# A layer's first two transfers cut anew: norm weights, one weight tile and the left half of x first

## The chip, the cores and the metric

The kernel runs on one core of a Trainium2 chip. The metric is the device time of one execution in microseconds (us). Besides it there is one profiled execution, with its own time and a span from the first to the last instruction.

## The reference, cut to what matters

One layer of a hybrid encoder: x is 512 positions by 1024 features, float32.

```python
h = rms_norm(x, attn_norm_g)
xr, gate, q, k, v = split(h @ w_in)             # 2560 columns
y_rnn  = (rg_lru(conv(xr), fwd) + rg_lru(conv(xr), bwd)) * gelu(gate)
y_attn = dilated_attention(q, k, v, rel_bias)   # 8 heads, three windows
x = x + concat(rms_norm(y_rnn), rms_norm(y_attn)) @ w_out
x = x + square(relu(rms_norm(x) @ w_up)) @ w_down
return rms_norm(x, final_norm_g)
```

The change concerns the start: x times the norm weights `attn_norm_g`, and the first columns of `w_in` (those of `xr`), which are multiplied first. The row's own factor 1/sqrt(mean(x^2)) is applied later, to the products.

## The kernel before, in words

**Products in three passes.** Each float32 operand is split into a rounded part (`hi`) and the rest (`lo = value - hi`), both held in a type that TensorE multiplies at full pace. A product is hi*hi + hi*lo + lo*hi, three matmuls into the same bank (`mm3`, L311 to L314). ScalarE mostly does the rounding, VectorE the subtraction.

**Row tiles.** x comes transposed: 8 row tiles of 128 features, each 128 partitions by 512 positions. With row tile k come rows of `w_in`: 3 weight tiles of 128 columns (the first 384 columns of `xr`), side by side in one piece of memory, so that one transfer brings both: 512 + 384 = 896 columns (`xw`, L341). Row tile 0 has its own array `xw0` with the 8 columns of norm weights between x and the weights, and comes in two transfers: x and norm weights (520 columns, L335), then the three weight tiles (384, L336). A fourth weight tile (columns 384 to 511) is needed early for row tile 0 alone; it comes from `w_in[3]` by a third transfer of 128 columns (`w03`, L339). All of these are issued by the Sync queue (SP) in the order of the code; `vt` (small vectors) and row tile 7 follow.

**`cvx(k)`** (L347) scales x by the norm weights and rounds it into `h_hi`, rounds the weights into `w3h`, and subtracts both to get `h_lo` and `w3l`. For row tiles 0 and 1 the work is shared: for row tile 0 ScalarE rounds the left 256 columns of x (L353) and VectorE the right 256 (L354), VectorE two weight tiles (L356) and ScalarE the third (L357), then the fourth (L366). `sq(k)` (L370) squares x on ScalarE for the row sums, `addsq` (L374) adds the squares on VectorE. Each engine takes its instructions in the order in which the code calls them.

**TensorE** begins with 8 matmuls on a constant (`pwarm`, L141), two instructions each, whose result nobody uses. Then, at L448 to L460, four banks `pxr[0..3]` gather the products. For row tiles 0 and 1 the passes are the outer loop: first hi*hi of weight tiles 0, 1, 2, then hi*lo of the three, then lo*hi (L453); for row tile 0 the fourth bank follows (L455, with the lines of `mm3`). From row tile 2 on, `mm3` per tile. After that come the gates, the attention with its tables, the output projection, and the two halves of the large feed-forward part with streamed weights.

**The end.** `fg` (final norm weights) is read into `fgt[0]` and `fgt[1]`, 128 partitions each, in pieces of partitions given by `FGP` (L1356, issue at L1725): 3 pieces and 4.

Of the kernel before, what the change touches and what calls it, by code (L numbers as in the profile page):

```python
# [35 lines left out]
TH = S // 2  # L36
# [62 lines left out]
def hybrid_kernel(ctx: ExitStack, tc, xw0, xw, xn, w_in, w_v, w_out, w_up, w_dn, gates, vecs, bias, fg, out):  # L99
    nc = tc.nc  # L100
# [3 lines left out]
    work = ctx.enter_context(tc.tile_pool(name="work", bufs=1))  # L104
# [17 lines left out]
    def f(t):  # L122
        return t.bitcast(FT)
# [14 lines left out]
    act(warm, epsb, AF.Exp)  # L138
    pwarm = ps_("pwarm", "et")
    one = nc.const_aps.tensor(1.0, [P, P], FT)  # L140
    for _ in range(8):  # L141
        nc.tensor.matmul(pwarm[:, :P], lhsT=one, rhs=one, start=True, stop=True)

    def softplus_consts():
# [166 lines left out]
    def mm3(o, a, b, first, last, on=False):  # L311
        nc.tensor.matmul(o, lhsT=a[0], rhs=b[0], start=bool(first), stop=False, skip_group_check=on)  # L312
        nc.tensor.matmul(o, lhsT=a[0], rhs=b[1], start=False, stop=False, skip_group_check=on)  # L313
        nc.tensor.matmul(o, lhsT=a[1], rhs=b[0], start=False, stop=bool(last), skip_group_check=on)  # L314
# [8 lines left out]
    h_hi = big.tile([P, KD, S], FR, name="h_hi", tag="bigA")  # L323
    h_lo = big.tile([P, KD, S], FR, name="h_lo", tag="bigB")

    XW, XG = S + 3 * P, S + KD
    ag = consts.tile([P, KD], FT, name="ag")
    xwt, w3 = [], []
    for k in range(KD):
        if 4 <= k < 7:  # L330
            xwt.append(stream.tile([P, 1024], FT, name="wraw", tag="wraw", bufs=3)[:, :XW])
        else:
            xwt.append(work.tile([P, 1024], FT, name="tw", tag="tw", bufs=4)[:, :XW if k else XG + 3 * P])
        if k == 0:
            nc.sync.dma_start(xwt[0][:, :XG], xw0[:, :XG])  # L335
            nc.sync.dma_start(xwt[0][:, XG:], xw0[:, XG:])  # L336
            nc.gpsimd.tensor_copy(ag, xwt[0][:, S:XG])
            w03 = g_("w03")[:, :P]
            nc.sync.dma_start(w03, w_in[3][:, :P])  # L339
        else:  # L340
            nc.sync.dma_start(xwt[k], xw[k - 1])  # L341
        if k == 6:
            nc.sync.dma_start(vt, vecs)

    sqx = {}

    def cvx(k):  # L347
        x, w = xwt[k][:, :S], xwt[k][:, S if k else XG:]
        g = ag[:, k:k + 1] if k else xwt[0][:, S:S + 1]
        hi, lo = g_("w3h", FR), g_("w3l", FR)  # L350
        if k < 2:
            c = (2 * P, 3 * P)[k]
            act(h_hi[:, k, :c], x[:, :c], AF.Copy, scale=g)  # L353
            nc.vector.tensor_scalar(h_hi[:, k, c:], x[:, c:], g, None, op0=OP.mult)  # L354
            if k == 0:
                nc.vector.tensor_copy(hi[:, :2 * P], w[:, :2 * P])  # L356
                act(hi[:, 2 * P:3 * P], w[:, 2 * P:], AF.Copy)  # L357
            else:
                nc.vector.tensor_copy(hi[:, :3 * P], w)
        else:  # L360
            act(h_hi[:, k, :], x, AF.Copy, scale=g)
            act(hi[:, :3 * P], w, AF.Copy)
        stt(h_lo[:, k, :], x, g, f(h_hi)[:, k, :], op0=OP.mult, op1=OP.subtract)
        nc.vector.tensor_tensor(lo[:, :3 * P], w, f(hi)[:, :3 * P], op=OP.subtract)
        if k == 0:
            act(hi[:, 3 * P:], w03, AF.Copy)  # L366
            nc.vector.tensor_tensor(lo[:, 3 * P:], w03, f(hi)[:, 3 * P:], op=OP.subtract)
        w3.append((hi, lo))

    def sq(k):  # L370
        sqx[k] = g_("sqx")
        act(sqx[k], xwt[k][:, :S], AF.Square)

    def addsq(k):  # L374
        nc.vector.tensor_tensor(sqx[0], sqx[0], sqx.pop(k), op=OP.add)
# [72 lines left out]
    pxr = {t: ps_("pxr", "pj") for t in range(4)}  # L448
    for k in range(KD):
        if k < 2:  # L450
            for i, (a, b) in enumerate(((0, 0), (0, 1), (1, 0))):
                for t in range(3):
                    nc.tensor.matmul(pxr[t], lhsT=wk(t, k)[a], rhs=hk(k)[b], start=i == 0 and k == 0, stop=False)  # L453
            if k == 0:
                mm3(pxr[3], wk(3, 0), hk(0), True, False)  # L455
            continue
        for t in range(3):
            mm3(pxr[t], wk(t, k), hk(k), False, k == KD - 1)
            if k == KD - 1 and t == 0:
                sqt = turned(sqx[0], "et")  # L460

# [797 lines left out]
    for w in OSEQ:  # L1259
        for i in range(4):  # L1260
            tt, k = i // 2, i % 2
# [260 lines left out]
    for half in range(2):  # L1522
# [5 lines left out]
        start = 0  # L1528
        if half == 0:
            start = 3  # L1530
# [286 lines left out]
```

## Time and profile before

| | us |
|---|---|
| median of 3 runs | 525.29 (525.0 to 525.39) |
| profiled execution, its time | 525.49 |
| profiled execution, its span | 523.7 |
| TensorE (PE) busy | 517.1 (99% of the span) |
| VectorE (DVE) busy | 430.4 (82%) |
| ScalarE (ACT) busy | 352.2 (67%) |
| GpSimd (POOL) busy | 65.3 (12%) |

The time is that of the execution; the span runs from its first to its last instruction, 1.8 us less. PE stands for TensorE's matmuls, PEld for its weight loads, which run beside them, SP for the Sync engine, whose q marks its issuing queue. In a row of the timeline the first number is the start in us from the span's start, the second the duration, then engine, line, operation, and output<-inputs by the program's names; `x3` says that three like instructions were merged, and a bracket names idle time in front and what ended it. A matmul row's duration holds its way through the array, so two rows overlap, and the pace is read from one start to the next. Where a helper records every operation, the line is that of the helper (L312 to L314).

### The profile page before, as it was taken

To read this page: it belongs to the slowest core of one execution; us is meant where nothing else is said; L and a number is where in the kernel's file an instruction comes from. 1 tells how busy PE (TensorE), PEld (TensorE's weight loads), DVE (VectorE), ACT (ScalarE), POOL (GpSimd) and SP (SyncE) were. 2 spreads that over 40 slices of the span, in tenths; PEclk is the share of its full clock that TensorE was granted. 3 is DMA by queue.
4 is the path that set the end of the run, shared out by engine and by line. 5 is a ranking of instruction groups with operands and counts; after the bars stand their busy time and mean duration, and the time that the engine had idled before them with its cause. 6 is when DMAs were issued, how large, how long until landed. Compare 5 with 4: busy or idle time off the path is not lost.

```text
span 523.7 us, 8216 instructions
## 1 busy us (share of the span) xinstructions
PE 517.1 (99%) x3021; PEld 444.3 (85%) x3021; DVE 430.4 (82%) x668; ACT 352.2 (67%) x570; POOL 65.3 (12%) x89
## 2 busy tenths in 40 slices
PE   9999999999999999999999999999999999999995
PEld 8867888778777788899999888889999999888884
DVE  6899986788886898898789987789766978986885
ACT  7579946667857857586578666565667577655655
POOL 0173000000000321001300312001100300131000
PEclk9999999999999999999999999999999999999999
DMA  7636555266796499947595899976986497799704
GB/s 288 208 99 196 161 160 180 83 191 199 190 294 197 115 196 247 353 134 195 139 223 143 213 273 281 306 271 161 300 256 168 117 224 210 157 289 257 195 1 161
DMA packets 40329, 105.15 MB, mean 201 GB/s; under 512 B 5056, under 2 KB 13376, under 8 KB 40288
## 3 DMA queue, kind: packets, MB, share of 16 engines
q1 hardware_dynamic: 32448, 78.10, 44.5%
q0 software_dynamic: 7696, 26.32, 27.3%
q8 instruction: 24, 0.39, 0.3%
q10 hardware_dynamic: 144, 0.20, 0.1%
q14 instruction: 17, 0.14, 0.1%
HBM read 95.59 MB, written 4.29 MB: 191 GB/s over the span
## 4 chain that ended last, share of the span: by engine, by line
PE 99%; DVE 0%; issue 0%; DVEq 0%; ACT 0%; ACTq 0%
PE pu L314 10%; PE pu L312 10%; PE pu L313 10%; PE pd L314 10%; PE pd L312 10%; PE pd L313 10%; PE pqk L312 3%; PE pqk L314 3%; PE pqk L313 3%; PE pwo L312 3%; PE pwo L314 3%; PE pwo L313 3%; PE pav L942 2%; PE pt L842 2%; PE ps L806 2%; PE pp L312 1%
## 5 line engine op out<-in xcount | busy, mean ns | idle before, releaser
L269 DVE TENSOR_TENSOR wlo<-wraw,whi 128x1024 fp32r<-128x1024 f32 x71 | 86.6, 1220 | 24.0 <-ACT whi L247 23.9
L247 ACT ACTIVATE whi<-wraw 128x1024 fp32r<-128x1024 f32 x67 | 70.8, 1057 | 37.4 <-PE pd L314 18.4
L313 PE MATMUL pd<-wlo,ah 128*128 128x512 f32 (+1 forms) x195 | 75.2, 386 | 0.0
L312 PE MATMUL pd<-whi,ah 128*128 128x512 f32 (+1 forms) x195 | 75.2, 386 | 0.0
L314 PE MATMUL pd<-whi,al 128*128 128x512 f32 (+1 forms) x195 | 75.2, 386 | 0.0
L313 PE MATMUL pu<-hl,whi 128*128 128x256 f32 x224 | 63.4, 283 | 0.0
L314 PE MATMUL pu<-hh,wlo 128*128 128x256 f32 x224 | 63.4, 283 | 0.0
L312 PE MATMUL pu<-hh,whi 128*128 128x256 f32 x224 | 63.4, 283 | 0.0
L312 PE MATMUL pu<-h2h,whi 128*128 128x256 f32 (+1 forms) x200 | 60.1, 300 | 0.0
L313 PE MATMUL pu<-h2l,whi 128*128 128x256 f32 (+1 forms) x200 | 60.0, 300 | 0.0
L314 PE MATMUL pu<-h2h,wlo 128*128 128x256 f32 (+1 forms) x200 | 60.0, 300 | 0.0
L269 DVE TENSOR_TENSOR wlo<-tw,whi 128x1024 fp32r<-128x1024 f32 x37 | 45.2, 1221 | 17.7 <-ACT whi L247 17.7
L247 ACT ACTIVATE whi<-tw 128x1024 fp32r<-128x1024 f32 x38 | 40.1, 1058 | 24.9 <-PE pd L314 6.3
L312 PEld LDWEIGHTS pu<-hh,whi 128*128 128x128 f32 x224 | 43.0, 192 | 0.0
L313 PEld LDWEIGHTS pu<-hl,whi 128*128 128x128 f32 x224 | 43.0, 192 | 0.0
L314 PEld LDWEIGHTS pu<-hh,wlo 128*128 128x128 f32 x224 | 43.0, 192 | 0.0
L313 PEld LDWEIGHTS pd<-wlo,ah 128*128 128x128 f32 x195 | 36.6, 188 | 7.4
L312 PEld LDWEIGHTS pd<-whi,ah 128*128 128x128 f32 x195 | 36.6, 188 | 7.3
L314 PEld LDWEIGHTS pd<-whi,al 128*128 128x128 f32 x195 | 36.6, 188 | 7.4
L247 ACT ACTIVATE whi<-ts 128x1024 fp32r<-128x1024 f32 x24 | 25.4, 1060 | 25.2 <-PE pd L314 16.4
L313 PEld LDWEIGHTS pu<-h2l,whi 128*128 128x128 f32 x200 | 38.3, 191 | 1.3
L314 PEld LDWEIGHTS pu<-h2h,wlo 128*128 128x128 f32 x200 | 38.3, 191 | 1.3
(280 smaller groups left out, 1220.1 us busy)
## 6 DMA issues: line engine op xcount, KB each, us to landing
wraw<-in_w_up_dram SPq DMA_DIRECT2D x25, 512.0 KB, 4.8
ts<-in_w_dn_dram POOLq DMA_DIRECT2D x24, 512.0 KB, 13.5
wraw<-in_w_dn_dram SPq DMA_DIRECT2D x24, 512.0 KB, 8.7
tw<-in_w_up_dram SPq DMA_DIRECT2D x15, 512.0 KB, 6.7
tw<-in_w_up_dram POOLq DMA_DIRECT2D x15, 512.0 KB, 7.5
wraw<-in_w_in_dram SPq DMA_DIRECT2D x13, 512.0 KB, 4.3
ts<-in_w_dn_dram SPq DMA_DIRECT2D x8, 512.0 KB, 9.0
tw<-in_w_dn_dram SPq DMA_DIRECT2D x8, 512.0 KB, 7.0
```

Of the source, the lines that this page charges most:

```text
L247: act(hi, raws[i], AF.Copy)
L269: nc.vector.tensor_tensor(lo, r, f(splits[i][0]), op=OP.subtract)
L312: nc.tensor.matmul(o, lhsT=a[0], rhs=b[0], start=bool(first), stop=False, skip_group_check=on)
L313: nc.tensor.matmul(o, lhsT=a[0], rhs=b[1], start=False, stop=False, skip_group_check=on)
L314: nc.tensor.matmul(o, lhsT=a[1], rhs=b[0], start=False, stop=bool(last), skip_group_check=on)
L806: nc.tensor.matmul(psq[p, u][e][:, :NK], lhsT=qs_[p, a][r, P * qt:P * qt + P], rhs=kks[p][r, b, w:w + NK], start=i == 0, stop=i == 2)
L842: nc.tensor.transpose(pt[:, i * P:(i + 1) * P], en[h][qt][:, k:k + P], ident)
L942: nc.tensor.matmul(pav[p][a, co], lhsT=vs[:, jt, h * DH:(h + 1) * DH], rhs=et[h, jt][:, ci], start=jt == 0 and i == 0, stop=jt == 3 and i ...
```

## The change

Row tile 0's array is put in another order and its transfers are cut elsewhere. The first transfer now brings the norm weights, weight tile 0 and the left half of x (8 + 128 + 256 = 392 columns), the second the right half of x and weight tiles 1 and 2 (512 columns). The fourth weight tile of row tile 0 is appended to row tile 1's transfer (1024 columns instead of 896), and its own transfer goes. `cvx(0)` deals its work out anew: VectorE rounds the left half of x, ScalarE weight tile 0, VectorE tiles 1 and 2, ScalarE the right half; the subtractions are made for each half of x and for tile 0 and tiles 1 and 2 apart. `cvx(1)` gets the rounding and subtraction of the fourth tile ahead of its own. The hi*hi products of row tile 0 are made by column halves: the left 256 columns of weight tiles 0, 1, 2, then the right 256. There are 7 warm-up matmuls instead of 8, and `fgt[0]` is read in 4 pieces instead of 3. In the code P is 128, S is 512, TH is 256 and KD is 8; `lr` holds the two column halves; the line numbers of the changed kernel are 5 to 14 higher from here on.

```diff
-    for _ in range(8):
+    for _ in range(7):
...
-    XW, XG = S + 3 * P, S + KD
+    XW, X0 = S + 3 * P, KD + P
+    XL, XR = X0 + TH, X0 + S + 2 * P
...
-            nc.sync.dma_start(xwt[0][:, :XG], xw0[:, :XG])
-            nc.sync.dma_start(xwt[0][:, XG:], xw0[:, XG:])
-            nc.gpsimd.tensor_copy(ag, xwt[0][:, S:XG])
-            w03 = g_("w03")[:, :P]
-            nc.sync.dma_start(w03, w_in[3][:, :P])
+            nc.sync.dma_start(xwt[0][:, :XL], xw0[:, :XL])
+            nc.sync.dma_start(xwt[0][:, XL:], xw0[:, XL:XR])
+            nc.gpsimd.tensor_copy(ag, xwt[0][:, :KD])
+        elif k == 1:
+            nc.sync.dma_start(xwt[1], xw0[:, XR:])
...
+        if k == 0:
+            wa, wb = xwt[0][:, KD:X0], xwt[0][:, X0 + S:]
+            nc.vector.tensor_scalar(h_hi[:, k, lr[0]], x[:, lr[0]], g, None, op0=OP.mult)
+            act(hi[:, :P], wa, AF.Copy)
+            nc.vector.tensor_copy(hi[:, P:3 * P], wb)
+            act(h_hi[:, k, lr[1]], x[:, lr[1]], AF.Copy, scale=g)
+            for c in lr:
+                stt(h_lo[:, k, c], x[:, c], g, f(h_hi)[:, k, c], op0=OP.mult, op1=OP.subtract)
+            nc.vector.tensor_tensor(lo[:, :P], wa, f(hi)[:, :P], op=OP.subtract)
+            nc.vector.tensor_tensor(lo[:, P:3 * P], wb, f(hi)[:, P:3 * P], op=OP.subtract)
+        elif k == 1:
+            c = 3 * P
+            w03, hi0, lo0 = xwt[1][:, XW:], w3[0][0][:, c:], w3[0][1][:, c:]
+            act(hi0, w03, AF.Copy)
             act(h_hi[:, k, :c], x[:, :c], AF.Copy, scale=g)
             nc.vector.tensor_scalar(h_hi[:, k, c:], x[:, c:], g, None, op0=OP.mult)
...
+            nc.vector.tensor_tensor(lo0, w03, f(hi0), op=OP.subtract)
+            nc.vector.tensor_copy(hi[:, :3 * P], w)
...
+                if i == k == 0:
+                    for c in lr:
+                        for t in range(3):
+                            nc.tensor.matmul(pxr[t][:, c], lhsT=wk(t, 0)[0], rhs=hk(0)[0][:, c], start=c is lr[0], stop=False, skip_group_check=True)
+                    continue
...
-    FGP = ((0, 32, 64, 128), (0, 32, 64, 96, 128))
+    FGP = ((0, 32, 64, 96, 128), (0, 32, 64, 96, 128))
```

TensorE's queue at the start, before (`pwarm` is the warm-up, `w3h` and `w3l` the rounded weights and their rest, `h_hi` and `h_lo` the same of x, `pxr` the banks; in brackets the engines or transfers whose semaphores a row waits for):

```order
L142 MATMUL pwarm<-const-float32-1.0 128x128 x8
L453 MATMUL pxr<-h_hi,w3h 128x512 [waits DVE_49,Activation_49]
L453 MATMUL pxr<-h_hi,w3h 128x512
L453 MATMUL pxr<-h_hi,w3h 128x512 [waits Activation_49]
L453 MATMUL pxr<-h_lo,w3h 128x512 [waits DVE_49]
L453 MATMUL pxr<-h_lo,w3h 128x512 x2
L453 MATMUL pxr<-h_hi,w3l 128x512 [waits DVE_49]
L453 MATMUL pxr<-h_hi,w3l 128x512 x2
L312 MATMUL pxr<-h_hi,w3h 128x512 [waits Activation_49]
L313 MATMUL pxr<-h_lo,w3h 128x512
L314 MATMUL pxr<-h_hi,w3l 128x512 [waits DVE_49]
```

and now:

```order
L142 MATMUL pwarm<-const-float32-1.0 128x128 x7
L464 MATMUL pxr<-h_hi,w3h 128x256 [waits DVE_49,Activation_49]
L464 MATMUL pxr<-h_hi,w3h 128x256 [waits DVE_49]
L464 MATMUL pxr<-h_hi,w3h 128x256
L464 MATMUL pxr<-h_hi,w3h 128x256 [waits Activation_49]
L464 MATMUL pxr<-h_hi,w3h 128x256 x2
L467 MATMUL pxr<-h_lo,w3h 128x512 [waits DVE_49]
L467 MATMUL pxr<-h_lo,w3h 128x512 x2
L467 MATMUL pxr<-h_hi,w3l 128x512 [waits DVE_49] x2
L467 MATMUL pxr<-h_hi,w3l 128x512
L312 MATMUL pxr<-h_hi,w3h 128x512 [waits Activation_49]
L313 MATMUL pxr<-h_lo,w3h 128x512
```

Three products of 512 columns have become six of 256, of which the first waits for VectorE and ScalarE once, the second for VectorE again and the fourth for ScalarE again; the passes behind them stand as they stood.

ScalarE's queue, before (`tw` and `w` are what the transfers brought, `ag` the copied norm weights, `sqx` the squares; DMAHW0, 1, 2 and so on are the Sync transfers in the order of issue):

```order
L353 ACTIVATE h_hi<-tw 128x256 [waits DMAHW0_49]
L357 ACTIVATE w3h<-tw 128x128 [waits DMAHW1_49]
L366 ACTIVATE w3h<-w_102 128x128 [waits DMAHW2_49]
L372 ACTIVATE sqx<-tw 128x512
L353 ACTIVATE h_hi<-tw,ag 128x384 [waits DMAHW3_49,Pool_49]
L372 ACTIVATE sqx<-tw 128x512
L361 ACTIVATE h_hi<-tw,ag 128x512 [waits DMAHW4_49]
L362 ACTIVATE w3h<-tw 128x384
```

and now:

```order
L356 ACTIVATE w3h<-tw 128x128 [waits DMAHW0_49]
L358 ACTIVATE h_hi<-tw 128x256 [waits DMAHW1_49]
L381 ACTIVATE sqx<-tw 128x512
L366 ACTIVATE w3h<-tw 128x128 [waits DMAHW2_49]
L367 ACTIVATE h_hi<-tw,ag 128x384 [waits Pool_49]
L381 ACTIVATE sqx<-tw 128x512
L372 ACTIVATE h_hi<-tw,ag 128x512 [waits DMAHW3_49]
L373 ACTIVATE w3h<-tw 128x384
```

The fourth weight tile's rounding (L366) stood ahead of the squares of row tile 0 and waited for a transfer of its own; it stands behind them now and waits for row tile 1's transfer, in front of that tile's own rounding.

The Sync queue, before (the row's last number is the transfer's partitions by columns):

```order
L335 DMA tw<-in_xw_dram 128x520
L336 DMA tw<-in_xw_dram 128x384
L339 DMA w_102<-in_w_in_dram 128x128
L341 DMA tw<-in_xw_dram 128x896 x3
L341 DMA wraw<-in_xw_dram 128x896 x3
L343 DMA vt<-in_vecs_dram 128x60
L341 DMA tw<-in_xw_dram 128x896
```

and now:

```order
L336 DMA tw<-in_xw_dram 128x392
L337 DMA tw<-in_xw_dram 128x512
L340 DMA tw<-in_xw_dram 128x1024
L342 DMA tw<-in_xw_dram 128x896 x2
L342 DMA wraw<-in_xw_dram 128x896 x3
L344 DMA vt<-in_vecs_dram 128x60
L342 DMA tw<-in_xw_dram 128x896
```

One issue has gone, and row tile 1's transfer is the third instead of the fourth.

More of the change, by code (lines that the diff above doesn't have):

```diff
@@ L362, in cvx @@
             act(hi[:, :3 * P], w, AF.Copy)
[L363 to L367, printed above, removed]
+        if k:
+            stt(h_lo[:, k, :], x, g, f(h_hi)[:, k, :], op0=OP.mult, op1=OP.subtract)
+            nc.vector.tensor_tensor(lo[:, :3 * P], w, f(hi)[:, :3 * P], op=OP.subtract)
         w3.append((hi, lo))
@@ L371, in sq @@
         sqx[k] = g_("sqx")
-        act(sqx[k], xwt[k][:, :S], AF.Square)
+        act(sqx[k], xwt[k][:, :S] if k else xwt[0][:, X0:X0 + S], AF.Square)
     def addsq(k):
@@ L451, in hybrid_kernel @@
             for i, (a, b) in enumerate(((0, 0), (0, 1), (1, 0))):
+                if i == k == 0:
[3 more added lines that the diff above has]
+                    continue
                 for t in range(3):
-                    nc.tensor.matmul(pxr[t], lhsT=wk(t, k)[a], rhs=hk(k)[b], start=i == 0 and k == 0, stop=False)
+                    nc.tensor.matmul(pxr[t], lhsT=wk(t, k)[a], rhs=hk(k)[b], start=False, stop=False, skip_group_check=True)
             if k == 0:
@@ L457, in hybrid_kernel @@
         for t in range(3):
-            mm3(pxr[t], wk(t, k), hk(k), False, k == KD - 1)
+            mm3(pxr[t], wk(t, k), hk(k), False, k == KD - 1, True)
             if k == KD - 1 and t == 0:
```

20 lines of the change are left out of this document (7 added, 13 removed).

## The prediction

> **What bounds the kernel now.** I read the page first (engine shares, then the chain that ended last), then TensorE's waits, then the first 16 us of the timeline, because every edit but one lies there, and last the groups by line and the DMA issues for durations.
>
> ```profile
> span 523.7 us, 8216 instructions
> PE 517.1 (99%) x3021; PEld 444.3 (85%) x3021; DVE 430.4 (82%) x668; ACT 352.2 (67%) x570; POOL 65.3 (12%) x89
> ...
> PE 99%; DVE 0%; issue 0%; DVEq 0%; ACT 0%; ACTq 0%
> ```
> TensorE is busy for 517.1 of 523.7 us and 99% of the chain that ended last is its own work. So what ends last is TensorE's queue from its first instruction to nearly its last; whatever makes that queue start its real products earlier shifts everything behind it, and nothing else does.
>
> ```profile
> PE pwarm L142 <- PEq L1806: 0.8, 1, 0.8
> PEld pxr L453 <- ACT w3h L357: 0.2, 1, 0.2
> ```
> The first row is the only wait of TensorE's matmul side in the whole span (0.8 us, before the warm-up). The second is the one wait of its weight loads at the place of the change: 0.2 us on the first rounded weight tile. Now the start itself (start, duration, engine, line):
>
> ```profile
> 0.73 0.39 SPq L335 DMA_DIRECT2D tw<-in_xw_dram  x1
> 0.77 3.75 PE L142 MATMUL pwarm<-const-float32-1.0 128*128 128x128 f32 x16 [0.77 <-PEq L1806]
> 1.18 0.41 SPq L336 DMA_DIRECT2D tw<-in_xw_dram  x1
> 1.64 0.42 SPq L339 DMA_DIRECT2D w<-in_w_in_dram  x1
> ...
> 3.50 0.36 DVE L354 TENSOR_SCALAR h_hi<-tw 128x256 fp32r<-128x256 f32 x1 [2.65 <-DMA tw<-in_xw_dram]
> 3.50 0.51 ACT L353 ACTIVATE h_hi<-tw 128x256 fp32r<-128x256 f32 x1 [1.27 <-DMA tw<-in_xw_dram]
> ...
> 4.00 0.31 ACT L357 ACTIVATE w3h<-tw 128x128 fp32r<-128x128 f32 x1
> 4.00 0.29 DVE L356 CAST w3h<-tw 128x256 fp32r<-128x256 f32 x1
> 4.21 0.74 DVE L363 SCALAR_TENSOR_TENSOR h_lo<-tw,h_hi 128x512 fp32r<-128x512 f32 x1
> 4.41 0.93 PEld L453 LDWEIGHTS pxr<-h_hi,w3h 128*128 128x128 f32 x3 [0.18 <-ACT w3h L357]
> 4.44 1.62 PE L453 MATMUL pxr<-h_hi,w3h 128*128 128x512 f32 x3
> ...
> 5.30 0.31 ACT L366 ACTIVATE w3h<-w 128x128 fp32r<-128x128 f32 x1 [0.99 <-DMA w<-in_w_in_dram]
> ...
> 5.64 0.29 DVE L367 TENSOR_TENSOR w3l<-w,w3h 128x128 fp32r<-128x128 f32 x1 [0.22 <-ACT w3h L366]
> 5.85 1.34 PE L453 MATMUL pxr<-h_lo,w3h 128*128 128x512 f32 x3
> ...
> 6.50 0.62 ACT L353 ACTIVATE h_hi<-tw,ag 128x384 fp32r<-128x384 f32 x1 [0.38 <-DMA tw<-in_xw_dram]
> ...
> 7.03 0.84 PE L453 MATMUL pxr<-h_hi,w3l 128*128 128x512 f32 x3
> ...
> 7.71 0.39 PE L312 MATMUL pxr<-h_hi,w3h 128*128 128x512 f32 x1
> ...
> 8.39 0.84 PE L453 MATMUL pxr<-h_hi,w3h 128*128 128x512 f32 x3
> ```
> The reader is to see three things. First, x and the norm weights arrive at 3.50, the weights at 4.00, and the first real weight load goes out at 4.41, 0.1 us behind the rounding that ended at 4.31 (4.00 + 0.31). Second, TensorE is slow here: the three products of 512 columns that begin at 4.44 give way to the next three at 5.85, and three later ones take 7.03 to 7.71, 0.227 us each. Third, from 5.85 on no row stands behind a wait.
>
> ```profile
> L142 PEld LDWEIGHTS pwarm<-const-float32-1.0 x16: 286/333/333, 0.7 to 3.9; 128*128 128x128 f32 x16
> L142 PE MATMUL pwarm<-const-float32-1.0 x16: 421/421/551, 0.8 to 4.1; 128*128 128x128 f32 x16
> L453 PEld LDWEIGHTS pxr<-h_hi,w3l x6: 187/188/277, 6.7 to 10.0; 128*128 128x128 f32 x6
> ```
> The weight loads tell when the slow time ends: 333 ns in the warm-up, 277 ns for the load at 6.71, 187 ns after it. The products show the same: if two of the three that begin at 5.85 take a slow step and the third a mixed one, the change of pace is at about 6.85. A slow step is 0.43 us (5.85 less 4.44 is 1.41 for three, of which about 0.14 is the first load's fill), nearly twice 0.227. The warm-up is sixteen instructions from 0.8 to 4.1, so 0.22 apart: eight matmuls end at about 4.3, seven at about 3.87.
>
> **The change part by part.**
>
> *The first two transfers.* The first shrinks from 260 KB (520 columns) to 196 KB (392), the second grows from 192 KB to 256 KB (512). Together both are 904 columns, as before.
>
> ```profile
> tw<-in_xw_dram SPq DMA_DIRECT2D x1, 260.0 KB, 2.7
> tw<-in_xw_dram SPq DMA_DIRECT2D x1, 192.0 KB, 2.8
> w<-in_w_in_dram SPq DMA_DIRECT2D x1, 64.0 KB, 3.6
> 2.50:3.50 1.00, 1.00 (x7) 1.00 (x7) 0.00 (x0) 0.00 (x0) 0.00 (x0) 1.00 1.03 360
> ```
> In the stretch in which they arrive the DMA engines are full (share 1.03) and move 360 GB/s. So 64 KB less is 65,536 / 360,000 = 0.18 us: the first lands so that its readers start at 3.32 instead of 3.50. The second ends with the same total byte, and I take 4.00 for its readers, as now. Its bounds: 0.18 later (bigger packets, started no earlier) and 0.2 earlier (it starts as much earlier as the first ends).
>
> *The first product.* ScalarE rounds the first weight tile (0.31, as L357) from 3.32 to 3.63, VectorE the left half of x (0.36, as L354) to 3.68. With one warm-up matmul less TensorE is free at 3.87. So the first half product (256 columns, half of 0.43: 0.21 cold) runs from about 3.9 to 4.1. The second and third need the two tiles that VectorE rounds at 4.00 (0.29, as L356) to 4.29; their load goes out at 4.41, just where the first one stands now. So TensorE arrives at 4.41 with one of six half products behind it: a lead of 0.21 us in slow time. From there the rest is the same work: five halves and then the same chain. Splitting three products into six adds three weight loads; I take nothing for them, because in the warm-up loads follow each other every 0.22 us beside matmuls as short as these halves. If they did not hide, they would cost up to 3 x 0.33 us less the 0.21 of each that streams, 0.36 slow us.
>
> *What the lead is worth.* Slow time ends at 6.85 as now. 0.21 us of slow stream is half a product, and at the full pace half a product is 0.227 / 2 = 0.11 us. That is the gain, and it holds to the end only if nothing behind it is late. That is checked next, each with the new need 0.2 us earlier before 6.85 and 0.11 after.
>
> *The other rounding of tile 0.* ScalarE does the right half of x (0.51, as L353) from 4.00 to 4.51; the fourth half product needs it at 4.57 + 2 x 0.21 = 4.99. VectorE now has two subtractions of 256 columns instead of one of 512 (0.74):
>
> ```profile
> L1473 DVE SCALAR_TENSOR_TENSOR x1n<-pd,r,x1n x1: 484/484/484, 516.8 to 516.8; 128x256 f32<-128x256 f32 x1
> L1476 DVE TENSOR_TENSOR tw<-x1n,fgt x1: 414/414/414, 517.6 to 517.6; 128x256 f32<-128x256 f32 x1
> ```
> At 0.48 each they end at 5.25, needed at about 5.64; then 0.29 (128 columns, as L367) to 5.54 and 0.41 (256) to 5.95, needed at 5.64 + 3 x 0.43 = 6.92. Slack 0.4 and 1.0 us.
>
> *The fourth tile in row tile 1's transfer.* The 64 KB transfer goes (one issue of 0.42 us on the Sync queue); its bytes ride in the next one, issued at 1.64 instead of 2.11, so by bytes that one lands no later than now (readers at 6.50). Rounding and subtraction of the fourth tile move behind it: ScalarE 6.50 to 6.81, then its 384 columns (0.62) to 7.43 instead of 7.12; VectorE 0.29 more. TensorE wants the fourth tile at 7.71 - 0.11 = 7.60 and row tile 1 at 8.28: slack 0.8 and 0.7. Behind the inserted instructions stand row tiles 2 to 7, each up to 0.5 us later:
>
> ```profile
> 8.31 0.75 DVE L363 SCALAR_TENSOR_TENSOR h_lo<-tw,ag,h_hi 128x512 fp32r<-128x512 f32 x1
> 10.05 0.74 DVE L363 SCALAR_TENSOR_TENSOR h_lo<-tw,ag,h_hi 128x512 fp32r<-128x512 f32 x1
> ...
> 10.43 0.39 PE L312 MATMUL pxr<-h_hi,w3h 128*128 128x512 f32 x1
> ...
> 12.47 0.39 PE L312 MATMUL pxr<-h_hi,w3h 128*128 128x512 f32 x1
> ```
> VectorE needs 1.74 us a row tile, TensorE 2.04, so the cover grows by 0.3 with each. For row tile 2 it is least: VectorE's subtractions would begin at about 8.8 and end (0.75 + 0.55) at 10.1, wanted at 10.77. Cost nothing; if that cover were gone, each 0.1 us over it would be 0.1 us of the total.
>
> *The fg load.* One issue more of four, before the last stage, on the Sync queue:
>
> ```profile
> L1725 SPq DMA_DIRECT2D fgt<-in_fg_dram x7: 311/441/825, 463.8 to 470.5; - x7
> L1466 DVE SCALAR_TENSOR_TENSOR ot<-x1n,rf,fgt x3: 752/752/752, 511.1 to 515.0; 128x512 f32<-128x512 f32 x3
> ```
> It is issued by 471 and first read at 511.1: 40 us of cover for one more issue of at most 0.83 us. Nothing. With the 64 KB issue gone and this one added, the number of Sync transfers stays.
>
> *Sum.* The profiled execution took 525.49 us, 1.8 more than its span; 525.49 - 0.11 = 525.38. It is 0.2 above the median of the runs, 525.29, on which scale the forecast is 525.29 - 0.11 = 525.18, say 525.2.
>
> *A rule against it.* The slow pace ends about 6.1 us after TensorE's first instruction, in a stretch in which it rested little: from 4.31 to 4.41 or, counted by the stream, 4.57. With the change it rests from 4.1 to the same place, 0.21 us more. The Trainium skill, "TensorE: Matmul & The Clock Gate" (The HAM clock gate), says that the clock is granted after a busy window of about 3.4 us, that these windows run free of the kernel, and that the moment varies with where the kernel falls in them. The trace agrees with a doubling of pace, but it came 6.1 us after the start, later than one such window; by windows of that length one of them would have begun near 3.45 and held both the old rest and the new one.
>
> **The rivals.**
>
> *The lead is eaten (same).* If the bigger second transfer lands 0.18 later, the second product's load goes out at 4.59 and the lead shrinks to 0.03; with loads that do not hide it turns into a loss of 0.3 slow us, 0.17 in the end. 525.3 to 525.5. For it: packets of 2,048 bytes instead of 1,536 behind a queue that issues only every 0.45 us. Against it: the engines are full, so bytes decide. The change then does what it says, and it is worth nothing.
>
> *The pace changes later (slower).* The rest in front of the second product is 0.21 longer and the stretch before it is a warm-up matmul shorter. If that is enough for the pace not to change at 6.85, the next chance decides. If the count begins anew with the second product at 4.57, the change comes 6.1 us on, at 10.67, 3.82 us later; in that time TensorE does 0.227 / 0.43 = 53% of its work, so 3.82 x 0.47 = 1.80 us are lost: 525.2 + 1.8 = 527.0. With the skill's window of 3.4 us it would be 1.6, an estimate from that page. It decides as soon as the tolerated rest is between 0.26 us (what it tolerates now) and 0.47.
>
> *The pace changes sooner (faster).* If the moment hangs not on the kernel but on when it was started, any execution may have it up to some us sooner. To pass 0.2% it must come 2 us sooner: 2 x 0.47 + 0.11 = 1.05. 2.5 us sooner gives 524.0. Against it: the three runs and the profiled execution lie within 0.5 us (525.0 to 525.49), so the moment wandered by about 1 us at most.
>
> **How the numbers follow.** 0.2% is 1.05 us, about what a measurement of this kernel can tell from no change. The forecast (lead of 0.11 kept) has 0.69, the eaten lead 0.14, the later pace 0.12, the sooner pace 0.05. So within 0.2% is 0.83, slower 0.12, faster 0.05. The range: down, 525.0 (fastest run) less 0.22 (lead of 0.41 slow us if the second transfer is 0.2 early) less 0.2 for a moment that moves by half a microsecond: 524.6. Up, 525.5 for the eaten lead and 0.47 for a moment 1 us later: 526.0. That leaves out the two rivals of the pace, 0.17.
>
> **What would show it.** Right: the first product's weights go out before 3.95, a rest of about 0.3 us, the second's load at 4.41 +/- 0.1, the three low-part products 0.2 us earlier than 5.85, loads of 187 ns from about 6.9 on, the first product of row tile 1 at 8.28, row tile 2 at 10.32 and no new wait of TensorE behind it. Wrong: the second load later than 4.6 (transfer), loads of 333 ns after 7.1 (pace), a wait of the fourth tile's products near 7.6 or of row tile 1 near 8.3 (the moved rounding was on the path), or a difference that first appears after 20 us.

## The result, and the profile after

| | before | after |
|---|---|---|
| median, us | 525.1 (524.52 to 525.6, 22 runs) | 525.87 (525.28 to 526.51, 22 runs) |
| profiled execution, its time | 525.49 | 525.8 |
| profiled execution, its span | 523.7 | 524.0 |

The change makes the kernel slower by 0.77 us: ratio 1.0015, 95% interval 1.0008 to 1.0021. The forecast was 0.11 us faster, at 525.2. The time lies in the range of 524.6 to 526.0, but it moved, and in the other direction. One further run of before, at 570.47 us with a granted clock of 0.851, was a slow one and is left out of every figure.

The page of after, its span, its busy times and the chain that ended last:

```profile
span 524.0 us, 8216 instructions
PE 516.1 (98%) x3022; PEld 443.2 (85%) x3022; DVE 430.4 (82%) x670; ACT 352.3 (67%) x570; POOL 65.4 (12%) x89
...
PE 97%; DMA 1%; DVE 0%; SPq 0%; ACT 0%; issue 0%; DVEq 0%; ACTq 0%
```
TensorE is busy 1.0 us less, and the span is 0.3 longer. The chain, before all TensorE, has 1% of DMA in it. Where that 1% lies, the chain of the first 12 us shows (start, duration, what), of before and then of after:

```profile
by line: PE pxr L453 45.0%; PE pwarm L142 31.3%; PE pxr L312 7.6%; PE pxr L313 5.7%; PE pxr L314 5.7%; issue 0.4%
...
0.77 3.75 PE pwarm L142 x16
4.52 3.35 PE pxr L453 x9
```

```profile
by line: DMA tw<-in_xw_dram 47.2%; PE pxr L467 17.3%; PE pxr L312 8.0%; PE pxr L313 5.8%; PE pxr L314 5.7%; SPq L337 3.4%; SPq L336 3.2%; ACT w3h L366 2.6%; issue 2.0%
...
1.64 5.67 DMA tw<-in_xw_dram
...
7.33 0.32 ACT w3h L366
...
7.69 0.50 PE pxr L312
```
Before, the chain was TensorE's own queue from the warm-up on. After, it runs through the transfer with row tile 1 and the fourth tile, from its issue at 1.64 to its landing at 7.31, then through the rounding of the fourth tile. TensorE's timeline and the readers of the transfers, of after:

```profile
3.27 0.31 ACT L356 ACTIVATE w3h<-tw 128x128 fp32r<-128x128 f32 x1 [1.05 <-DMA tw<-in_xw_dram]
3.27 0.37 DVE L355 TENSOR_SCALAR h_hi<-tw 128x256 fp32r<-128x256 f32 x1 [2.41 <-DMA tw<-in_xw_dram]
3.75 0.19 PEld L464 LDWEIGHTS pxr<-h_hi,w3h 128*128 128x128 f32 x1
3.78 0.35 PE L464 MATMUL pxr<-h_hi,w3h 128*128 128x256 f32 x1
3.96 0.29 DVE L357 CAST w3h<-tw 128x256 fp32r<-128x256 f32 x1 [0.32 <-DMA tw<-in_xw_dram]
4.17 0.88 DVE L360 SCALAR_TENSOR_TENSOR h_lo<-tw,h_hi 128x256 fp32r<-128x256 f32 x2
4.30 0.66 PEld L464 LDWEIGHTS pxr<-h_hi,w3h 128*128 128x128 f32 x5 [0.37 <-DVE w3h L357]
4.31 0.86 PE L464 MATMUL pxr<-h_hi,w3h 128*128 128x256 f32 x5 [0.17 <-DVE w3h L357]
5.10 0.96 PE L467 MATMUL pxr<-h_lo,w3h 128*128 128x512 f32 x3
5.90 0.85 PE L467 MATMUL pxr<-h_hi,w3l 128*128 128x512 f32 x3
7.33 0.31 ACT L366 ACTIVATE w3h<-tw 128x128 fp32r<-128x128 f32 x1 [2.35 <-DMA tw<-in_xw_dram]
7.69 0.50 PE L312 MATMUL pxr<-h_hi,w3h 128*128 128x512 f32 x1 [0.94 <-ACT w3h L366]
...
8.50 0.85 PE L467 MATMUL pxr<-h_hi,w3h 128*128 128x512 f32 x3
...
10.57 0.40 PE L312 MATMUL pxr<-h_hi,w3h 128*128 128x512 f32 x1
```

The waits of the first 12 us in after (in total, times, longest):

```profile
PEld pxr L312 <- ACT w3h L366: 1.4, 1, 1.4
PE pxr L312 <- ACT w3h L366: 0.9, 1, 0.9
PEld pxr L464 <- DVE w3h L357: 0.4, 1, 0.4
```
Two things are to be seen. First, TensorE runs at the quick pace from the second product on: the three products that begin at 5.10 are 0.27 us apart on the mean, where before the three that begin at 4.44 were 0.47 apart. The trace's record of the clock has the change of pace at 3.64 in this execution and at 6.89 in the profiled one of before. Second, TensorE can't use the time won: the last of its nine products begins at about 6.36, it could take the fourth tile at about 6.6, and it gets it at 7.69. Row tile 2's first product begins at 10.57 after 10.43, and from there the two executions run at a fixed distance. The same two products of the last stage, the second of them TensorE's last, before and after:

```profile
515.32 0.39 PE L314 MATMUL pd<-whi,al 128*128 128x512 f32 x1
...
517.58 0.28 PE L314 MATMUL pd<-whi,al 128*128 128x256 f32 x1
```

```profile
515.48 0.39 PE L314 MATMUL pd<-whi,al 128*128 128x512 f32 x1
...
517.73 0.28 PE L314 MATMUL pd<-whi,al 128*128 128x256 f32 x1
```
515.48 less 515.32 is 0.16, and at row tile 2 it was 0.14. So between row tile 2 and TensorE's last product nothing of the change acts. An execution that was given the quick pace 3.25 us sooner lost all that this was worth while TensorE stood.

The rest of the spans' difference, 0.17, lies behind the last product, and it comes with the change. From the start of that product to the end of the span it is 6.14 us in before and 6.31 in after. Of the 18 profiles of this document, the nine of kernels that read row tile 1 from the end of row tile 0's array have 6.28 to 6.31 there, the other nine 6.10 to 6.15, with three pieces of `fg` or with four; the means differ by 0.16. What comes later is the end of the last output transfer: the last of its sixteen completion marks comes 5.38 to 5.40 us after the start of the last product in the first nine and 5.19 to 5.24 in the others, though it is issued at 2.73 to 2.74 in all of them. Why the longer array delays that mark, no run shows.

### The profile page after: what moved, and what is told of

It is laid out like the page before. It is cut to its first block, busy times and chain, and to the rows that moved or that the text cites. A ratio compares the mean times of both kernels' runs of the same rounds, so it can differ in the third digit from the quotient of the medians.

```text
span 524.0 us, 8216 instructions
## 1 busy us (share of the span) xinstructions
PE 516.1 (98%) x3022; PEld 443.2 (85%) x3022; DVE 430.4 (82%) x670; ACT 352.3 (67%) x570; POOL 65.4 (12%) x89
## 4 chain that ended last, share of the span: by engine, by line
PE 97%; DMA 1%; DVE 0%; SPq 0%; ACT 0%; issue 0%; DVEq 0%; ACTq 0%
PE pu L313 10%; PE pu L314 10%; PE pu L312 10%; PE pd L313 10%; PE pd L312 10%; PE pd L314 10%; PE pqk L312 3%; PE pqk L314 3%; PE pqk L313 3%; PE pwo L312 3%; PE pwo L314 3%; PE pwo L313 3%; PE pav L956 2%; PE pt L856 2%; PE ps L820 2%; PE pp L312 1%
## 5 line engine op out<-in xcount | busy, mean ns | idle before, releaser
L312 PEld LDWEIGHTS pu<-h2h,whi 128*128 128x128 f32 x200 | 38.3, 191 | 1.3
```

## The experiments

The letters in the expectations: A is the theory that TensorE stands for the fourth tile, which comes with row tile 1's bytes; C that the merged transfer lands later than row tile 1's did and that TensorE waits for it; D that the array with the longer rows is the cost; B the rival of the forecast that the pace changes later; W, at the end, that the whole loss is waiting for data in the first 11 us; E that it lies in the instructions themselves or elsewhere. In the table the moment of the change of pace is from the trace's record of the clock, and "row tile 1 read" is the start of the first instruction that reads that transfer, both in us of the one profiled execution. "Long" means that row tile 1 is read from the end of row tile 0's array, in rows of 7,712 bytes, "own" that it is read from an array of rows of 3,584 or 4,096 bytes.

| kernel | first cut | row tile 1 | fourth tile | median (runs), us | ratio to before, 95% | pace changes | row tile 1 read |
|---|---|---|---|---|---|---|---|
| before | old | own | apart | 525.05 (108) | | 6.89 | 6.50 |
| again | old | own | apart | 525.72 (1) | | 6.33 | 6.14 |
| long1 | old | long | apart | 525.69 (11) | 1.0004 to 1.0022 | 4.33 | 6.86 |
| sep1 | old | own | merged | 525.38 (11) | 0.9998 to 1.0016 | 6.20 | 7.23 |
| only4 | old | long | merged | 525.69 (11) | 1.0005 to 1.0022 | 4.99 | 7.48 |
| own4x | new | own | apart | 525.37 (11) | 0.9999 to 1.0017 | 3.61 | 6.84 |
| own4 | new | long | apart | 525.60 (11) | 1.0003 to 1.0022 | 4.77 | 6.70 |
| aftersep | new | own | merged | 525.81 (11) | 1.0003 to 1.0021 | 5.45 | 6.72 |
| after | new | long | merged | 525.87 (22) | 1.0008 to 1.0021 | 3.64 | 7.33 |
| warm8 | new | long | merged | 525.90 (11) | 1.0006 to 1.0023 | 6.01 | 7.10 |
| skip4 | new | long | merged | 525.82 (11) | 1.0006 to 1.0023 | 3.81 | 7.41 |
| late4 | new | long | apart, behind | 525.47 (11) | 1.0001 to 1.0018 | 5.15 | 6.46 |
| late0 | old | own | apart, behind | 525.26 (11) | 0.9993 to 1.0012 | 5.05 | 6.51 |

**The parts taken apart.** *own4* is after with the fourth tile by its own transfer, issued third as before:

```diff
-            nc.sync.dma_start(xwt[1], xw0[:, XR:])
+            nc.sync.dma_start(w03, w_in[3][:, :P])
+            nc.sync.dma_start(xwt[1], xw0[:, XR:XR + XW])
```

> The changed kernel with one part undone: the fourth weight tile comes by its own transfer again, third in the queue, row tile 1's transfer is 896 columns, the rounding and subtraction of the fourth tile stand where they stood before, and fg has 3 pieces (so that the count of transfers is that of before). Theory A (the fourth tile arrives with row tile 1's bytes at about 7.3 instead of 5.3, and TensorE, which comes to it at 6.6, stands 1.4 us): the loss of 0.77 us goes, 524.9 to 525.2, and the trace has no wait of a pxr load longer than 0.5 us besides the one in front of the second half product. Theory B (the longer rest in front of the second half product, or one warm-up matmul less, moves the change of pace): the rest is still there, so about 525.9.

Measured: 525.60, between the two, as neither A nor B has it. In its profile, at the quick pace from 4.77, TensorE stands mostly at row tile 2, which ScalarE can read only at 8.68:

```profile
8.68 0.72 ACT L373 ACTIVATE h_hi<-tw,ag 128x512 fp32r<-128x512 f32 x1 [0.84 <-DMA tw<-in_xw_dram]
...
9.87 0.50 PE L312 MATMUL pxr<-h_hi,w3h 128*128 128x512 f32 x1
...
11.05 0.40 PE L312 MATMUL pxr<-h_hi,w3h 128*128 128x512 f32 x1
```
The three products from 9.87 to 11.05 take 1.18 us instead of 0.68.

*only4* is before with nothing but the merged transfer, read from the long array as in after (and the four pieces of `fg`):

```diff
-            nc.sync.dma_start(w03, w_in[3][:, :P])
-            nc.sync.dma_start(xwt[1], xw[0])
+            nc.sync.dma_start(xwt[1], xw0[:, XG + 3 * P:])
```

> The kernel before with this part alone: the fourth weight tile appended to row tile 1's transfer (1024 columns), rounded and subtracted ahead of row tile 1; fg in 4 pieces. First transfers, 8 warm-ups and products of 512 columns as before. A: slower than before by 0.5 to 1.0 us, 525.6 to 526.1, with a wait of the fourth bank's first load on the rounding of the fourth tile. B: the rest and the warm-up are those of before, so 525.1.

Measured: 525.69, most of the loss without the new cut. Its timeline shows the same standing as after (in the bracket the idle time and what ended it):

```profile
7.48 0.31 ACT L355 ACTIVATE w3h<-tw 128x128 fp32r<-128x128 f32 x1 [2.63 <-DMA tw<-in_xw_dram]
7.84 0.50 PE L312 MATMUL pxr<-h_hi,w3h 128*128 128x512 f32 x1 [0.83 <-ACT w3h L355]
```

*warm8* is after with eight warm-ups, which takes away the longer rest in front of the second product:

```diff
-    for _ in range(7):
+    for _ in range(8):
```

> The changed kernel with 8 warm-up matmuls instead of 7. A: TensorE stands for the fourth tile all the same, 525.7 to 526.0. B: the rest in front of the second half product shrinks by 0.4 us and the change of pace comes when it came before, so at most 525.3.

Measured: 525.90, as after. *again* is the kernel before, for a second profile:

> The kernel before once more, for a second profile: where does the change of pace fall in another execution? A: it may fall anywhere between about 3.6 and 7; where it falls early, TensorE comes early to the fourth bank, finds the fourth tile there (landed by 5.3) and waits for row tile 1 at about 6.5 to 7.1 instead; row tile 2's first product at about 9.7 to 10.4. B: near 6.9 as in the first profile, with row tile 2's first product at 10.4.

Measured: one run of 525.72. Its change of pace came at 6.33, half a microsecond sooner than in the first profile, and its time was no better, because now TensorE had to wait within the products of row tile 2:

```profile
8.89 0.72 ACT L361 ACTIVATE h_hi<-tw,ag 128x512 fp32r<-128x512 f32 x1 [1.62 <-DMA tw<-in_xw_dram]
...
10.15 0.43 PE L312 MATMUL pxr<-h_hi,w3h 128*128 128x512 f32 x1
10.45 0.50 PE L313 MATMUL pxr<-h_lo,w3h 128*128 128x512 f32 x1
10.92 0.50 PE L314 MATMUL pxr<-h_hi,w3l 128*128 128x512 f32 x1
11.26 0.40 PE L312 MATMUL pxr<-h_hi,w3h 128*128 128x512 f32 x1
```
From 10.15 on the products are 0.30, 0.47 and 0.34 apart instead of 0.227: 0.43 us lost, on a transfer that VectorE and ScalarE could read only at 8.89. So before, too, runs close to its transfers.

**Is it the fourth tile's own wait?** *skip4* makes the fourth tile's two parts out of the third, which is there already; its transfers are those of after.

```diff
+            act(hi[:, 3 * P:], wb[:, P:], AF.Copy)
+            nc.vector.tensor_tensor(lo[:, 3 * P:], wb[:, P:], f(hi)[:, 3 * P:], op=OP.subtract)
...
-            act(hi0, w03, AF.Copy)
...
-            nc.vector.tensor_tensor(lo0, w03, f(hi0), op=OP.subtract)
```

> The changed kernel, with the fourth tile's parts made from the third tile, which is there by 4.0 (so the fourth bank's products of row tile 0 are of wrong numbers): nothing waits for the fourth tile, the transfers are those of the changed kernel. Theory A, wait on the fourth tile: TensorE does the fourth bank's three products (0.68 us at full pace) while row tile 1 is under way and then waits for that alone: 0.4 to 0.7 us less than the changed kernel, 525.2 to 525.5. Theory C, row tile 1's late landing alone is the loss: 0.0 to 0.3 less, 525.6 to 525.9.

Measured: 525.82, no gain. The wait only moves from the fourth tile to row tile 1, which lands in the same transfer:

```profile
7.41 0.61 ACT L367 ACTIVATE h_hi<-tw,ag 128x384 fp32r<-128x384 f32 x1 [2.28 <-DMA tw<-in_xw_dram]
...
6.99 0.39 PE L314 MATMUL pxr<-h_hi,w3l 128*128 128x512 f32 x1
8.13 0.93 PE L466 MATMUL pxr<-h_hi,w3h 128*128 128x512 f32 x3 [0.75 <-ACT h_hi L367]
```
TensorE does the fourth bank's three products by 7.2 and stands until 8.13. At row tile 2 this execution is still 0.2 us ahead of that of after; it loses 0.41 at 418.8 us, waiting for a streamed weight of the feed-forward part, and whether its other runs do so too isn't known. So that skip4 gains nothing rests on the median of its eleven runs, and where the waiting goes rests on one profile.

**The array.** *own4x* is own4 with row tile 1 back in its old array, so that of the change only the cut, the dealing, the half products and seven warm-ups are left; *sep1* is only4 with the 1,024 columns in an array of their own.

```diff
-            nc.sync.dma_start(xwt[1], xw0[:, XR:XR + XW])
+            nc.sync.dma_start(xwt[1], xw[0])
```

> The kernel with the fourth tile's own transfer (own4), and row tile 1 read from the array of the others again as before, not from row tile 0's: of the change only the cut of the first two transfers, the new dealing, the half products and 7 warm-ups are left. Theory D (own4 stays slow because rows of 7,712 bytes in the long array land later): 525.0 to 525.2, row tile 1 landed by 6.4. If not D, the cut itself or the new dealing costs: 525.5 to 525.7.

```diff
-            nc.sync.dma_start(xwt[1], xw0[:, XG + 3 * P:])
+            nc.sync.dma_start(xwt[1], xw1)
```

> The kernel before with the fourth tile in row tile 1's transfer (only4), but the 1024 columns in an array of their own. D: row tile 1 lands by 6.5 and the loss of only4 (0.63 us) halves at least, 525.1 to 525.4. A without D: lands at 7.0 to 7.5 as in only4 and TensorE waits for the fourth tile, 525.6 to 525.9.

Measured: 525.37 and 525.38, each 0.2 to 0.3 below its partner with the long array, and each with an interval that holds no change. *long1* is the array alone: before, with row tile 1 at the end of row tile 0's rows, nothing merged.

```diff
-            nc.sync.dma_start(xwt[k], xw[k - 1])
+        elif k == 1:
+            nc.sync.dma_start(xwt[1], xw0[:, XG + 3 * P:XG + 3 * P + XW])
```

> The kernel before, except that row tile 1's 896 columns stand at the end of row tile 0's array (rows of 7,712 bytes) and are read from there; the transfers, their sizes and their order are those of before. Theory C (the merged transfer's late landing is the cost): the time of before, 525.1, row tile 1 landing at 6.0 to 6.6. Rival D (the long array is the cost): 525.4 to 525.5, the 0.25 to 0.3 us by which the kernels with an own array (525.37, 525.38) lay under those with the long one (525.6, 525.69). Between 525.2 and 525.35 the two can't be told apart.

Measured: 525.69. That is against C as the whole account: without a merged transfer the time is that of only4. In its profile TensorE, at the quick pace since 4.33, ends the fourth bank at 7.26 and then waits 0.3 us for row tile 1 (this execution took 525.22, less than the median, as did those in the profiles of own4x, 524.98, and aftersep, 525.05):

```profile
6.86 0.62 ACT L355 ACTIVATE h_hi<-tw,ag 128x384 fp32r<-128x384 f32 x1 [0.79 <-DMA tw<-in_xw_dram]
...
7.03 0.40 PE L314 MATMUL pxr<-h_hi,w3l 128*128 128x512 f32 x1
7.57 0.93 PE L455 MATMUL pxr<-h_hi,w3h 128*128 128x512 f32 x3
```

*aftersep* is the counterpart: after, with the 1,024 columns in an array of their own.

```diff
-            nc.sync.dma_start(xwt[1], xw0[:, XR:])
+            nc.sync.dma_start(xwt[1], xw1)
```

> The changed kernel, except that row tile 1 and the fourth tile (the same 1,024 columns, still one transfer) have an array of their own. Theory C: the transfer still ends at 7.0 to 7.4 and TensorE still stands in front of the fourth tile and row tile 1, so the time is that of after, 525.9, or at most 0.2 less. Rival D: the long array costs 0.25 to 0.3 of the 0.77, so 525.55 to 525.65.

Measured: 525.81, as C has it and not D. With long1, which went against C, this says that neither part alone is the cause. The first nine kernels of the table hold all eight ways of taking or leaving the three parts, and a part's effect is the mean of the four kernels with it less the mean of the four without. By the means of the runs that is +0.24 us for the new cut (95% interval by resampling 0.11 to 0.37), +0.28 for the long array (0.15 to 0.41) and +0.21 for the merge (0.09 to 0.34). Together 0.73; measured 0.77. Long1 and only4 show that they don't simply add: once one part is there, another may cost little more. Of the long array's 0.28, about 0.16 is the later end of the last output transfer, as the 18 profiles have it.

**Another order.** *late4* and *late0* issue the fourth tile's transfer behind row tile 1's and do its products after row tile 1's, late4 in own4, late0 in before.

```diff
-            nc.sync.dma_start(w03, w_in[3][:, :P])
             nc.sync.dma_start(xwt[1], xw0[:, XR:XR + XW])
+            nc.sync.dma_start(w03, w_in[3][:, :P])
...
-            if k == 0:
+            if k == 1:
                 mm3(pxr[3], wk(3, 0), hk(0), True, False)
```

> The changed kernel's first two transfers and half products, then row tile 1 (896 columns) third, the fourth tile by its own transfer behind it, and row tile 0's products of the fourth bank behind row tile 1's on TensorE. A: row tile 1 is not behind or with the fourth tile's bytes and lands 0.2 us sooner than in own4, but TensorE has 0.68 us less to do before it: 525.3 to 525.8. If it beat the kernel before (under 525.0), what counts would be row tile 1's landing alone (C).

> The kernel before, except that the fourth tile's own transfer is issued behind row tile 1's instead of ahead of it, and row tile 0's products for the fourth bank stand behind row tile 1's. Theory C says that the landing of row tile 1 decides in the executions in which the clock changes early: row tile 1 is issued 0.45 us sooner and lands at 5.6 to 6.2, so the time falls by 0.1 to 0.4, to 524.7 to 525.0, unless row tile 2, which lands at 7.5 to 8.9 in all profiles, takes its place at once; then it stays at 525.1. The rival that the order of the small transfers doesn't matter (only the total of the bytes ahead) gives 525.1 as well; a time over 525.3 speaks against both.

Measured: 525.47 and 525.26. Late4 is no better than own4 beyond the spread, late0 no better than before: the gain of 0.1 to 0.4 that C promised for late0 didn't come. Row tile 1 was read at 6.46 and 6.51 though it was issued one place sooner, as late as in the kernels with the small transfer ahead. No version beat before.

**All waits covered.** What the three parts share was tested by a cover: 24 more warm-up matmuls between row tile 0's nine products and the fourth bank's, in before (*padb*), in after (*pada*) and in own4x (*padx*).

```diff
             if k == 0:
+                for _ in range(24):
+                    nc.tensor.matmul(pwarm[:, :P], lhsT=one, rhs=one, start=True, stop=True)
                 mm3(pxr[3], wk(3, 0), hk(0), True, False)
```

> The kernel before with 24 more warm-up matmuls (same instruction and bank, nobody uses their result) between row tile 0's first nine products and the fourth bank's. At the quick pace they take about 24 x 0.11 = 2.6 us, in executions whose pace changes late up to about 3.5, so 527.3 to 528.6 in all. They push every later product back by more than TensorE has stood for a transfer in any profile so far (1.4), so that the landings of row tiles 1 and 2 can decide nothing. Alone it tells nothing; it is the measure for pada and padx.

> The changed kernel with the same 24 matmuls at the same place. Theory W (the whole 0.77 us is TensorE waiting in the first 11 us for data that land later): as quick as padb within 0.2, or 0.1 quicker by the lead of the first product. Rival E (the loss lies elsewhere: in the six half products, in more instructions, in the transfers at the end): 0.77 slower than padb, at least 0.5.

> The changed kernel's new cut, dealing, half products and seven warm-ups, with the fourth tile by its own transfer and row tile 1 in its old array as before, and the same 24 matmuls. Theory W: within 0.2 of padb, or 0.1 quicker. Rival E, with the 0.24 that the cut costs on the mean of the kernels with it and without, lying in the products themselves: 0.2 to 0.3 slower than padb.

Measured, four runs each: 530.72, 530.29, 529.92. The cover is twice as long as expected: each of these matmuls is two instructions of 0.11 us, so 48 of them, 5.2 us. The two kernels once more:

> padb once more, since four runs of each are few (padb 530.72, pada 530.29). Measure for pada2: 530.4 to 530.9.

> pada once more. Theory W: between 0.5 quicker and 0.1 slower than padb2; if the lead of 0.11 us that the forecast gave the first product is real under the cover, 0.1 to 0.2 quicker. Rival E: 0.5 to 0.8 slower.

Measured, four runs each: 530.28 and 530.33. Of eight runs each the medians are 530.53 without the change and 530.33 with it; the difference of the means is -0.06 us, 95% interval -0.40 to 0.28. The 0.77 is gone, and E, which asked for at least 0.5, is out. W holds for the start, though not for the whole 0.77: pada and pada2 have the later end of the last output transfer too (6.29 and 6.30 us behind TensorE's last product, against 6.14 in padb and padb2), and 0.16 is too little to be seen in this interval. Padx came out lower than W allowed: 529.92 is 0.80 below the first padb; against all eight runs of padb the means differ by -0.34, with an interval of -0.72 to 0.08. The rows of the first padb and pada show it in one execution each (the reader of row tile 1, the cover, the first product behind it):

```profile
6.64 0.62 ACT L353 ACTIVATE h_hi<-tw,ag 128x384 fp32r<-128x384 f32 x1 [0.45 <-DMA tw<-in_xw_dram]
...
6.68 5.08 PE L456 MATMUL pwarm<-const-float32-1.0 128*128 128x128 f32 x44
...
11.96 0.47 PE L312 MATMUL pxr<-h_hi,w3h 128*128 128x512 f32 x1
```

```profile
7.91 0.31 ACT L366 ACTIVATE w3h<-tw 128x128 fp32r<-128x128 f32 x1 [2.97 <-DMA tw<-in_xw_dram]
...
6.59 5.08 PE L470 MATMUL pwarm<-const-float32-1.0 128*128 128x128 f32 x44
...
11.87 0.47 PE L312 MATMUL pxr<-h_hi,w3h 128*128 128x512 f32 x1
```
In pada row tile 1 and the fourth tile can be read 1.27 us later than in padb, and the product behind the cover begins 0.09 sooner, by what TensorE led at the cover's start (6.59 to 6.68). Late data cost nothing once TensorE doesn't want them.

## Why the prediction was wrong, point by point

*What held.* The first transfer's readers start at 3.27 (forecast 3.32), the second's at 3.96 (4.00); the first half product goes out at 3.75 to 3.78 (3.9), the second's load at 4.30 (4.41). The four pieces of `fg` cost nothing that shows, and no new wait of TensorE appears behind 20 us.

*The lead of 0.11 us.* It was reckoned in slow time with "the pace changes at 6.85, as now". At the quick pace the slack of 0.4 us that I gave to VectorE's two subtractions of x is gone. The halves themselves run as priced: the last four of the five begin 0.12 apart, at 4.53, 4.65, 4.77 and 4.89, about half of 0.227, so the added weight loads cost next to nothing. TensorE could begin the second pass at about 5.00, but VectorE's second subtraction ends only at 5.05 (4.17 + 0.88), and the load behind it goes out at 5.10. The next product then begins 0.34 behind the first instead of 0.23, as it does behind TensorE's stop for the fourth tile (0.34 from 7.69). That is how the lead is eaten. After begins its second pass at 5.10, long1, with the old cut and the quick pace from 4.33, at 5.18. Under the cover the lead can't be told from nothing.

*The step that failed* is the fourth tile: "by bytes that one lands no later than now", and "TensorE wants the fourth tile at 7.60 and row tile 1 at 8.28: slack 0.8 and 0.7". Both halves of it were off.

The bytes were right, but they don't set the landing. Up to 6.40 us, when before had its row tile 1, both kernels have moved the same (last column GB/s, the mean over the 6.4 us; 1,350 KB and 1,338 KB):

```profile
0.00:6.40 6.40, 5.63 (x21) 5.09 (x22) 2.14 (x6) 3.12 (x6) 0.93 (x8) 1.00 0.66 211
```

```profile
0.00:6.40 6.40, 5.46 (x26) 4.90 (x26) 2.05 (x7) 2.83 (x5) 0.93 (x8) 1.00 0.66 209
```
All that was issued up to and with row tile 1 is 1,928 columns in either, 987 KB counted in the same way. A transfer is marked complete in the trace in sixteen parts: in after 14 of row tile 1's are there at 5.97, the last two at 6.96 and 7.31. In ten profiles with row tile 1 in a transfer by itself its first reader started between 6.14 and 6.86, in the eight with the merged one between 6.72 and 7.91; means of 6.53 and 7.29. The Trainium skill, "DMA: Bandwidth & Descriptors" (Why a DMA increments its semaphore by 16 and not by 1), says that a DMA runs on up to 16 engines that finish independently and that only the full count means that all data have landed. The trace agrees: the reader at 7.33 started behind the sixteenth mark. Why the last parts come later when the piece is 512 KB instead of 448 KB behind 64 KB, no run shows.

The slack was reckoned for one execution. In 18 profiles of these kernels the change of pace came anywhere between 3.61 and 6.89 us, and the profile from which I worked is the latest of them. With the quick pace from 3.64 TensorE wants the fourth tile at 6.6, a microsecond before the forecast's 7.60; the slack of 0.8 is then -0.2 even for a reader at 6.50, and -1.1 for the one that came. I had taken the narrow spread of three runs as a sign that the moment wanders "by about 1 us at most"; it wanders by 3.3, and what an early one brings is mostly given back to the transfers, which makes the times agree. That can be read from runs without a profile too, by their granted clock: in the profiles without a cover 0.997 stands beside changes of pace at 5.05 and 5.15, 0.998 beside changes from 5.45 to 6.33. The 28 runs of before with 0.997 have a mean of 524.93, the 53 with 0.998 one of 525.06, though a change of pace some 0.8 us sooner would be worth 0.4 if nothing waited. In after both groups (eight runs each) have 525.85 to 525.87. The Trainium skill, "TensorE: Matmul & The Clock Gate" (The HAM clock gate), calls the window free-running and gives the shift as 500 ns to either side; that it runs free agrees with these profiles, the size does not: 3.28 us from first to last, about one of its windows of 3.4. The length of the window shows in the record of the clock: in the 18 profiles TensorE has the quick pace for 515.41, 518.83 or 522.24 us without a break, which are 3.41 apart.

*The rivals.* The later pace (527.0) didn't come: after, warm8 and skip4 changed at 3.64, 6.01 and 3.81, none later than before. The eaten lead is half of what happened: it takes the gain away, but not 0.77 more; and neither of its two causes came, since the second transfer was read at 3.96 and the loads hid. The sooner pace did come and brought nothing, since the data weren't there. The rival that decided was not among them: the merged and moved row tile 1 as the place where TensorE stands, on which I had put a slack instead of a price.

*What stays open.* That the loss, all but the 0.16 behind the last product, is waiting for data in the first 11 us is shown by the cover, within its interval. How the longer array delays the end of the last output transfer isn't found. That the merged transfer is read later is shown by the readers. How the long array costs the rest of its 0.28 at the start is only suggested: with the transfer apart, the readers start at a mean of 6.67 (three profiles) with it and 6.47 (seven) without, merged at 7.40 (six) and 6.98 (two), which fits but is few. How the new cut costs its 0.24 isn't found: its readers of row tile 1 start no later than with the old one. Row tile 2 may: in the ten profiles with the fourth tile apart its last completion mark comes at a mean of 8.56 with the new cut (four, 8.16 to 8.94) and 8.03 with the old (six, 7.53 to 8.87), merged at 8.47 and 8.46, which again is few.

## What to carry to other kernels

Before a slack in the first microseconds is trusted, on TensorE or on an engine that feeds it, reckon it for the earliest change of pace among several profiles, not for the one at hand. A transfer is there when the last of its sixteen parts is there, so appending a piece that is wanted first to a larger one makes the small piece as late as the whole, whatever the bytes say. And a filler in front of the suspected wait, put into both kernels, tells whether a loss is waiting or work, once there are enough runs of both; what lies behind the last product has to be compared apart.

## What the runs showed that was not expected

The moment at which TensorE's pace doubles moved between 3.61 and 6.89 us over 18 profiles. The same 448 KB read from rows of 7,712 bytes instead of 3,584 made the kernel 0.6 us slower in long1 (525.69 against 525.05), and 0.28 on the mean over the four pairs; about 0.16 of it is at the other end of the kernel, in the last output transfer. One part of a transfer can lag far behind the other fifteen: in again row tile 2 had fifteen marks by 7.31 and the last at 8.87, and that part lagged by over 1.2 us in every transfer up to row tile 7's.
